# Matrix-engine order in an expert mixture: scheduled, or as the kernel writes it from the second pair of experts on

## The chip, the cores and the metric

The kernel runs on one core of a Trainium2 chip. The metric is device time in microseconds (us) of that core, from launch to end; each kernel is run several times and the median counts. A profile, taken of one execution, records every instruction. PE is TensorE (matrix engine), PEld its weight load, DVE VectorE, ACT ScalarE, POOL GpSimd, SP SyncE, which here issues the loads.

## The reference

A two-layer encoder on 512 tokens of 1024 channels, float32. Layer 0 mixes tokens by a Fourier transform and a convolution, layer 1 by banded attention; each layer ends with an expert-choice mixture of 16 experts, where each expert takes its own 64 tokens. The change is in the mixture:

```
def ec_moe(h, router_w, router_b, w_gate, w_up, w_down):
    aff = softmax(h @ router_w + router_b)
    gate, idx = top_k(aff transposed, 64)             # 64 tokens an expert
    xg = h[idx]                                       # 16 x 64 x 1024
    hid = silu(xg @ w_gate) * (xg @ w_up)             # 1024 x 1024 weights, each expert its own
    y = (hid @ w_down) * gate
    return zeros.at[idx].add(y)
...
x = x + gate_c * ec_moe(rms_norm(x) * (1 + scale) + shift, ...)
```

All three weight matrices of all 16 experts are read once a layer: 48 matrices of 4 MiB, 201.3 MB.

## The kernel before

`moe` (line 859) works through eight pairs of experts (`for pr in range(NP)`, line 1031). The two experts of a pair have 64 tokens each, so the 128 x 128 array is split in column halves: expert i = 0 uses columns 0 to 63, i = 1 columns 64 to 127. For a pair the source writes, in this order:

1. **gate**: `expert_mm` (line 965) with `wg_d`, into two banks of PSUM (one for each half of the 1024 outputs), then ACT's SiLU into `sg` (line 1040);
2. **combine** of the pair before (`combine_all`, line 1019): 16 matmuls that put the weighted outputs `Y` back on the tokens, which DVE adds to `x` (line 1017);
3. **up**: `expert_mm` with `wu_d`;
4. **ahead** (line 1044): `onehot` (DVE line 903, POOL line 909), `gather` (line 920; DVE line 928 and ACT line 926 empty its banks) and `weights` (lines 937 to 944) of the *next* pair;
5. DVE multiplies `up` with `sg` (line 1064), PE transposes the product (line 1069), `evac` (lines 151, 153) puts it into `hid`;
6. **down**: `expert_mm` with `wd_d`, then `y_out` (lines 1007 to 1009: DVE, ACT, DVE) forms `Y`.

The last pair's down projection is done in pieces (`down_piece`, line 981: one of 512 columns, two of 256), each followed by its part of combine.

One `expert_mm` has four steps of two chunks, one chunk for each expert; a chunk is 2 x 128 rows of a weight matrix, 1 MiB. Each step has eight matmuls, in the source with i = 0 and i = 1 by turns:

```
for kk in range(2):
    for h in range(2):
        for i in range(2):
            matmul(ps[h][64*i:64*i+64], lhs[:, k, 64*i:64*i+64], w[i].row(kk)[:, 512*h:512*h+512])
```

So a pair has 24 chunks, a layer 192; numbered from 0 in the order in which PE uses them, the second pair's up projection (`pr` = 1) begins with chunk 32 and the last pair's up projection ends with chunk 183.

`chunk` (line 100) issues each load on SP's queue, into one of the mixture's 15 slots of 1 MiB (`w0` to `w10`, `3a`, `3b`, `4a`, `4b`; `Slot`, line 54). Slots are handed out in rotation when the program is written, so a load waits on SP until PE has finished with the chunk that had the slot 15 places earlier, and all later loads wait behind it.

What the source fixes is which instructions there are and which data they depend on. The order on each engine is set by a scheduler that runs when the program is built (`schedule_with_timeline_sim=True`, line 1480): it plays the program through a model of the engines and issues on each engine what the model finds ready first. It is not bound to the source's order, for PE, DVE, ACT, POOL or SP.

Of the kernel before, what the change touches and what calls it, by code (L numbers as in the profile page):

```python
# [21 lines left out]
EPS = 1e-6  # L22
# [10 lines left out]
def trunk(ctx: ExitStack, tc: tile.TileContext, x_d, c_d, pos_d, ada_w, ada_b, mix_g, ffn_g, w_in,  # L33
# [7 lines left out]
    free_banks, free_slots = list(range(8)), [f"w{i}" for i in range(SLOTS)]  # L41

    class Bank:
        """One bank of PSUM, given back after its last use."""
# [9 lines left out]
    class Slot:  # L54
        """8 KB a partition, for a chunk of weights or parts of it, given back after its last use."""
# [14 lines left out]
    def area(i, n, dt=FT):  # L70
        """1a, 2a: 12 KB; 1b, 2b: 4 KB; 0a to 4b else: 8 KB, the 3s and 4s slots in the mixtures."""
        return pool.tile([P, n], dt, name=i if i[0] in "034" else f"area{i}")
# [6 lines left out]
    def row_tmp():  # L79
        """Of a slot lent for it, where there is one."""  # L80
        if not extra:
            return tmp()
        extra.append(extra.pop(0))
        return extra[-1]
# [15 lines left out]
    def chunk(src):  # L100
        """One chunk of weights in the order of the stream."""
        w = Slot()
        loads[0] = nc.sync.dma_start(w.cut(src.shape[1]), src)
        return w
# [7 lines left out]
    def halves(w, eng=None):  # L112
        """w = hi + lo exactly, both of 12 significant bits."""
# [10 lines left out]
    def behind(*ins):  # L124
        """Bulk work that its engines take up only after these instructions."""
# [13 lines left out]
    def mm3(ps, l, r, start, stop):  # L139
        """float32 product of (hi, lo) operands: the three parts above 2**-24."""  # L140
# [6 lines left out]
    def evac(out, in_):  # L147
        """PSUM to SBUF, by turns on the two engines that read PSUM."""
# [100 lines left out]
    def ada_steps(l, s, j, pool_too=False):  # L249
        """The same block in steps, on VectorE, or on ScalarE and GpSimd."""  # L250
# [45 lines left out]
    def row_half(p, col, h):  # L296
        """A half of a column vector of 1024 (128 x 8) as a row, the same on all partitions."""
# [11 lines left out]
    # the router's weights, 16 of 32 columns; the sum over the four groups of its rows  # L309
# [17 lines left out]
    def rsqrt(y, v, n, scale):  # L327
        """y = scale / sqrt(v): a guess from the bits, a step of third and one of second order."""
# [21 lines left out]
    def norm_rows(ss, name, parts=2, t0=0, n=TT):  # L350
        """1/sqrt(mean(x**2) + EPS) for some tiles of tokens, from the sums over parts of the channels"""
# [8 lines left out]
    def rms_row(rbc, ss, name, parts=2):  # L360
        """1/rms of the tokens as a row, the same on all partitions"""
# [7 lines left out]
    def h_area():  # L369
        """h as hi + lo, [128 channels, 512 tokens] eight times"""  # L370
# [3 lines left out]
    def h_parts(src, f, rbc, hi, lo, a, sh, k):  # L374
        """h = x*rbc*a + sh as hi + lo, x as [128 channels, 512 tokens]"""
# [4 lines left out]
    def fourths(*tags, dt=FT):  # L380
        """Areas as [128, 512] four times each"""
        return [m[:, S * k:S * k + S] for m in [area(i, 2048, dt) for i in tags] for k in range(4)]

    def turned_x():
        """x as [128 channels, 512 tokens] eight times"""
        return fourths("0a", "0b")
# [5 lines left out]
    def add_gated(t, h, ps, eng):  # L392
        """x += gate * y, of one token tile and one half of the channels."""
# [6 lines left out]
    def mixer0():  # L400
# [19 lines left out]
        # the first three chunks come by halves of their rows, the first halves ahead of the blocks 1 and 3  # L420
# [70 lines left out]
        def conv(ct, split):  # L491
            """Some taps on ScalarE and GpSimd, the others on VectorE"""
# [36 lines left out]
        def spectrum(g, u):  # L529
            """The real part of the transform of one group, u its projection"""  # L530
# [40 lines left out]
        # LayerNorm over the 512 channels, which lie across partitions  # L571
        ones = one.to_broadcast([P, 32])

        def sums(src):
            """Four rows (32 times each) of sums over the channels of four tiles"""
# [15 lines left out]
        # The order of the steps, one letter a kind (the branches below say which), its number, the engine or the  # L591
        # split of the step after a dot, the free slots that it picks after a colon.
# [122 lines left out]
    def prefix_matrices():  # L715
        """Rows j, columns i: 1 where j <= i; where j < i"""
# [9 lines left out]
    class Router:  # L726
# [20 lines left out]
        def part(self, t, h):  # L747
            """one tile of tokens, half of its channels: the sum of squares, the logits' part"""
# [17 lines left out]
        def affinities(self, t0, n):  # L766
            """softmax over the experts for some tiles of tokens, turned to a row an expert"""
# [34 lines left out]
        def tops(self, wk, out):  # L802
            """The 64 largest of a row, in steps"""
# [15 lines left out]
        def slots(self):  # L819
            """idx[token, expert]: 1..64, the token's place among the expert's, or 0  # L820

            Taken are the tokens above the 64th largest, and as many of its equals, the first ones, as are left."""
# [14 lines left out]
            with Bank() as p0, Bank() as p1:  # L837
                # counts of a mask up to each token (z = 0) and before it (z = 1)
# [20 lines left out]
    def moe(rt, last, meanwhile):  # L859
        l, a, sh, aff = rt.l, rt.a, rt.sh, rt.aff  # L860
        A0 = [area(i, 2048) for i in ("0a", "0b")]
        # the tokens as they come to the mixture: x itself until the first outputs are added to it
# [16 lines left out]
        def room():  # L879
            """For the transposed one-hot matrices and the weighted outputs."""  # L880
# [6 lines left out]
        def first_onehot():  # L887
            """The one of the first pair by its parts, straight with the factors."""
# [8 lines left out]
        def onehot(pr):  # L897
            """The one-hot matrix of a pair of experts."""
# [14 lines left out]
        def gather(pr, hf):  # L913
            """Half of the channels of the gathered rows of a pair of experts."""
# [569 lines left out]
```

## Time and profile before

| | us |
|---|---|
| median of 3 runs (1574.2 to 1575.35) | 1574.2 |
| profiled execution: span, first to last instruction | 1573.9 |
| of which PE busy | 1452.2 (92%) |
| DVE / ACT / POOL busy | 638.0 / 338.8 / 312.1 |
| share of the chain that ended last: PE / DVE | 78% / 16% |
| mixture of layer 0, from the first gather to the last piece's output | about 272 to 786 |
| mixture of layer 1, likewise | about 1052 to 1560 |

No time of the profiled execution apart from its span is recorded; the 0.3 us between its span and the median is less than the spread of the runs. A chain row gives start, length and what ran. A chain "x64" of line 976 stands for one `expert_mm`: 32 matmuls, each recorded as two rows. A window row gives for one stretch the busy time of each engine, then the clock granted to TensorE (1.00 is 2.4 GHz, 0.50 is 1.2 GHz), the DMA engines' busy share and the GB/s that they moved (the share can pass 1 by a little).

### The profile page before, as it was taken

What the parts mean: (1) busy time and instruction counts of PE and PEld (TensorE: products, weight loads), DVE (VectorE), ACT (ScalarE), POOL (GpSimd) and SP (SyncE); (2) the same over time, 40 slices, a digit from 0 to 9 for tenths busy, and PEclk for the clock granted to TensorE, in tenths of its full rate; (3) what the DMA queues carried; (4) which work ended last, traced back from release to release, by engine and by line L of the source; (5) the groups of instructions that cost most, each with busy time, mean ns of one, the idle gap of its engine ahead of it and who ended that gap; (6) DMA issues with size and microseconds to landing.
All of it is one profiled execution on the core that took longest, in us unless ns stands there. A gap on an engine that the chain in (4) does not pass through costs nothing.

```text
span 1573.9 us, 18049 instructions
## 1 busy us (share of the span) xinstructions
PE 1452.2 (92%) x7203; PEld 789.1 (50%) x7203; DVE 638.0 (41%) x1165; ACT 338.8 (22%) x686; POOL 312.1 (20%) x234
## 2 busy tenths in 40 slices
PE   5994897999999999999888989979999999999995
PEld 3762574544454444444467666654455344444443
DVE  5599946121221211211268888560222212212114
ACT  3443432210010000000255653411110010010002
POOL 2597631200000000000156655300000000000002
PEclk8997898999999999999989999979999999999998
DMA  9465389789998999999810476578999998999991
GB/s 339 141 221 182 128 316 405 303 330 403 410 401 343 355 383 362 412 362 406 276 36 14 120 228 199 213 310 321 386 390 412 410 378 318 409 362 404 371 388 69
DMA packets 158428, 480.69 MB, mean 305 GB/s; under 512 B 10416, under 2 KB 31176, under 8 KB 158344
## 3 DMA queue, kind: packets, MB, share of 16 engines
q1 hardware_dynamic: 158264, 479.27, 80.0%
q8 instruction: 57, 0.93, 0.2%
q0 software_dynamic: 80, 0.26, 0.0%
q14 instruction: 27, 0.22, 0.0%
HBM read 477.40 MB, written 2.10 MB: 305 GB/s over the span
## 4 chain that ended last, share of the span: by engine, by line
PE 78%; DVE 16%; ACT 2%; issue 1%; DMA 1%; SPq 0%; POOL 0%; ACTq 0%; DVEq 0%; POOLq 0%
PE bank L976 45%; PE bank L920 8%; DVE 0b L506 7%; PE bank L1014 4%; PE bank L141 3%; PE bank L142 3%; PE bank L143 3%; PE bank L997 2%; PE bank L227 2%; PE bank L1301 1%; DMA 4a<-in_fc_w_in_dram 1%; PE bank L942 1%; DVE nm L1271 1%; PE bank L1267 1%; PE bank L1292 1%
## 5 line engine op out<-in xcount | busy, mean ns | idle before, releaser
L976 PE MATMUL bank<-w,area2b 128*64 128x512 f32 x744 | 221.5, 598 | 0.0
L976 PE MATMUL bank<-w,area1b 128*64 128x512 f32 x688 | 207.3, 597 | 0.0
L976 PE MATMUL bank<-w,area1a 128*64 128x512 f32 x624 | 159.1, 594 | 0.9 <-ACT area2b L926 0.6
L909 POOL TENSOR_TENSOR tmp<-tmp,rr 128x512 f32<-128x512 f32 x14 | 17.7, 1265 | 650.6 <-DVE tmp L903 628.9
L1017 DVE TENSOR_TENSOR x<-x,bank 128x512 f32<-128x512 f32 (+1 forms) x136 | 81.1, 652 | 145.6 <-PE bank L1014 145.4
L976 PEld LDWEIGHTS bank<-w,area2b 128*64 128x64 f32 x744 | 67.8, 136 | 107.0 <-issue 101.7
L976 PEld LDWEIGHTS bank<-w,area1b 128*64 128x64 f32 x688 | 64.9, 136 | 106.0 <-issue 102.0
L1007 DVE SCALAR_TENSOR_TENSOR tmp<-bank,af,gbc 128x512 f32<-128x512 f32 (+1 forms) x34 | 24.5, 719 | 217.6 <-PE bank L976 191.1
L119 POOL TENSOR_TENSOR w<-w,w 128x1024 fp32r<-128x1024 f32 x30 | 75.5, 2536 | 148.7 <-ACT w L118 142.6
L1064 DVE TENSOR_TENSOR area1a<-bank,area1a 128x512 f32<-128x512 f32 x32 | 22.1, 691 | 198.0 <-PE bank L976 198.0
L976 PEld LDWEIGHTS bank<-w,area1a 128*64 128x64 f32 x624 | 55.7, 137 | 72.5 <-issue 68.5
L1014 PE MATMUL bank<-area2a 128*128 128x512 f32 (+1 forms) x272 | 73.4, 401 | 12.1 <-ACT area2a L1008 12.1
L1014 PEld LDWEIGHTS bank<-area2a 128*128 128x128 f32 x272 | 45.3, 188 | 56.7 <-ACT area2a L1008 22.2
L506 DVE SCALAR_TENSOR_TENSOR 0b<-3b,cw,0b 128x512 f32<-128x512 f32 x60 | 69.0, 1186 | 0.1
L920 PEld LDWEIGHTS bank<-tmp,0a 128*128 128x128 f32 x384 | 52.3, 191 | 33.4 <-issue 33.3
L1008 ACT ACTIVATE area2a<-tmp 128x512 fp32r<-128x512 f32 (+1 forms) x34 | 20.6, 607 | 219.7 <-DVE tmp L1007 219.7
L920 PE MATMUL bank<-tmp,0a 128*128 128x128 f32 x384 | 66.5, 286 | 0.0
L928 DVE TENSOR_SCALAR area1b<-bank,a,mod 128x128 f32<-128x128 f32 x32 | 13.1, 409 | 123.6 <-PE bank L920 118.7
L920 PE MATMUL bank<-tmp,0b 128*128 128x128 f32 x384 | 61.5, 279 | 0.0
L141 PE MATMUL bank<-area1a,w 128*128 128x512 f32 x132 | 52.8, 420 | 7.1 <-ACT area1a L377 6.3
L920 PEld LDWEIGHTS bank<-tmp,0b 128*128 128x128 f32 x384 | 51.2, 192 | 11.4 <-issue 11.4
L143 PE MATMUL bank<-area1a,w 128*128 128x512 f32 x132 | 53.4, 406 | 1.2 <-POOL w L119 1.2
(466 smaller groups left out, 2639.2 us busy)
## 6 DMA issues: line engine op xcount, KB each, us to landing
w<-in_moe_w_gate_dram SPq DMA_DIRECT2D x93, 1024.0 KB, 10.5
w<-in_moe_w_up_dram SPq DMA_DIRECT2D x86, 1024.0 KB, 12.9
w<-in_moe_w_down_dram SPq DMA_DIRECT2D x85, 1024.0 KB, 7.6
w<-in_ada_w_dram SPq DMA_DIRECT2D x44, 1024.0 KB, 7.0
3b<-in_moe_w_up_dram SPq DMA_DIRECT2D x10, 1024.0 KB, 13.9
4b<-in_moe_w_gate_dram SPq DMA_DIRECT2D x9, 1024.0 KB, 12.0
4a<-in_moe_w_gate_dram SPq DMA_DIRECT2D x9, 1024.0 KB, 10.6
3a<-in_moe_w_up_dram SPq DMA_DIRECT2D x9, 1024.0 KB, 11.8
```

What stands on the lines that cost most here:

```text
L119: eng.tensor_sub(lo.ap[:, s], w.ap[:, s], hi.ap[:, s].bitcast(FT))
L141: nc.tensor.matmul(ps, l[0], r[0], start=start, stop=False)
L142: nc.tensor.matmul(ps, l[0], r[1], start=False, stop=False)
L143: nc.tensor.matmul(ps, l[1], r[0], start=False, stop=stop)
L227: nc.tensor.matmul(ps[32 * q:32 * q + 32], cond[:, 4 * half + q], w[:, q], start=half == 0, stop=half == 1)
L506: nc.vector.scalar_tensor_tensor(cv, g[:, k:k + S], wt(k), cv, op0=OP.mult, op1=OP.add)
L920: nc.tensor.matmul(p[:, P * q:P * q + P], src_x(t, 4 * hf + q), oh[:, P * t:P * t + P], start=t == 0, stop=t == TT - 1)
L976: nc.tensor.matmul(ps[h][CAP * i:CAP * i + CAP], lhs[:, k, CAP * i:CAP * i + CAP], w[i].row(kk)[:, 512 * h:512 * h + 512], start=k == 0, s ...
L997: nc.tensor.matmul(ps[CAP * i:CAP * i + CAP, :n], lhs[:, k, CAP * i:CAP * i + CAP], w[i][:, kk], start=k == 0, stop=k == KT - 1)
L1007: nc.vector.scalar_tensor_tensor(f, ps[:, :n], af, gbc[:, s], op0=OP.mult, op1=OP.mult)
L1014: nc.tensor.matmul(p[:, :n], ohT[:, P * t:P * t + P], Y[z][:, c0:c0 + n], start=z == 0, stop=z == 1)
L1017: nc.vector.tensor_add(xx, xx, p[:, :n])
```

## The change

Around the loop over pairs, from `pr` = 1 to the end of the last pair's transposes, PE's instructions are put under a manual schedule: the scheduler keeps them, on PE alone, in the order in which the source writes them. The first pair, the pieces of the last down projection, and the other four engines remain with the scheduler, which, however, now plays its model with another PE. Both mixtures run through this code. The edit also takes out docstrings and comments, which issue nothing; lines after 1030 stand 3 to 4 lower.

```
         pend = None
+        order = ExitStack()
         for pr in range(NP):
+            if pr == 1:
+                order.enter_context(tc.manual_schedule(engines={mybir.EngineType.PE}))
             if pr:
                 xg, ohT, af = nxt
...
                             nc.scalar.activation(frozen[2 * t + h], xx, AF.Copy)
+        order.close()
         ss = small("fss", 3 * TT, 1)
```

What it moves, first on PE at the start of the fourth pair's gate projection in layer 0. (Left of the arrow stands the bank, right of it the weights and the gathered tokens `area2b`; `3b`, `w6` are chunks of expert i = 0, `w10`, `w3` of i = 1.) Before:

```order
L976 MATMUL bank3_2717<-3b_2719,area2b_1839 64x512
L976 MATMUL bank7_2718<-3b_2719,area2b_1839 64x512
L976 MATMUL bank3_2717<-w10_2721,area2b_1839 64x512
L976 MATMUL bank7_2718<-w10_2721,area2b_1839 64x512
L976 MATMUL bank3_2717<-3b_2719,area2b_1839 64x512
L976 MATMUL bank3_2717<-w10_2721,area2b_1839 64x512
L976 MATMUL bank7_2718<-3b_2719,area2b_1839 64x512
L976 MATMUL bank7_2718<-w10_2721,area2b_1839 64x512
L976 MATMUL bank3_2717<-w6_2731,area2b_1839 64x512
L976 MATMUL bank7_2718<-w6_2731,area2b_1839 64x512
L1014 MATMUL bank5_2769<-area2a_2010 128x512
L1014 MATMUL bank2_2777<-area2a_2010 128x512
```

With the change:

```order
L976 MATMUL bank3_2719<-3b_2721,area2b_1839 64x512
L976 MATMUL bank3_2719<-w10_2723,area2b_1839 64x512
L976 MATMUL bank7_2720<-3b_2721,area2b_1839 64x512
L976 MATMUL bank7_2720<-w10_2723,area2b_1839 64x512
L976 MATMUL bank3_2719<-3b_2721,area2b_1839 64x512
L976 MATMUL bank3_2719<-w10_2723,area2b_1839 64x512
L976 MATMUL bank7_2720<-3b_2721,area2b_1839 64x512
L976 MATMUL bank7_2720<-w10_2723,area2b_1839 64x512
L976 MATMUL bank3_2719<-w6_2733,area2b_1839 64x512
L976 MATMUL bank3_2719<-w3_2735,area2b_1839 64x512
L976 MATMUL bank7_2720<-w6_2733,area2b_1839 64x512
L976 MATMUL bank7_2720<-w3_2735,area2b_1839 64x512
```

Before, the two matmuls of `3b` stand together, then the two of `w10`, and after the first two of `w6` the combine of the pair before cuts in (line 1014). Now i = 0 and i = 1 alternate throughout, and combine and gather stand behind whole projections; PE's order on the change is the source's in every pair from the second on.

Second, on DVE late in layer 0's mixture, around the product of gate and up. Before:

```order
L1017 TENSOR_TENSOR x_61<-x_61,bank6_3587 128x512
L928 TENSOR_SCALAR area2b_1839<-bank2_3653,a01_119,mod01_108 128x128 x2
L928 TENSOR_SCALAR area2b_1839<-bank0_3674,a01_119,mod01_108 128x128 x2
L943 COPY af_3701<-bank6_3702 64x1
L944 COPY af_3701<-bank6_3702 64x1
L1017 TENSOR_TENSOR x_61<-x_61,bank3_3595 128x512
L1017 TENSOR_TENSOR x_61<-x_61,bank7_3591 128x512
L1064 TENSOR_TENSOR area1a_1837<-bank4_3599,area1a_1837 128x512
L1064 TENSOR_TENSOR area1a_1837<-bank5_3600,area1a_1837 128x512
L151 COPY area1a_1837<-bank7_3711 128x512
```

With the change (line 1064 is now line 1067):

```order
L1017 TENSOR_TENSOR x_61<-x_61,bank3_3597 128x512
L1067 TENSOR_TENSOR area1a_1837<-bank4_3601,area1a_1837 128x512
L1067 TENSOR_TENSOR area1a_1837<-bank5_3602,area1a_1837 128x512
L928 TENSOR_SCALAR area2b_1839<-bank2_3655,a01_119,mod01_108 128x128 x2
L928 TENSOR_SCALAR area2b_1839<-bank0_3676,a01_119,mod01_108 128x128
L943 COPY af_3703<-bank6_3704 64x1
L944 COPY af_3703<-bank6_3704 64x1
L928 TENSOR_SCALAR area2b_1839<-bank0_3676,a01_119,mod01_108 128x128
L151 COPY area1a_1837<-bank7_3713 128x512
```

Before, the gathered rows (line 928) are emptied ahead of the product; now the product stands first and the gather's banks are emptied behind it. All eight additions of combine stand ahead of both.

Third, SP's loads for the third pair in layer 0. Before:

```order
L103 DMA 4a_2573<-in_moe_w_up_dram 128x2x1024
L103 DMA 4b_2575<-in_moe_w_up_dram 128x2x1024
L103 DMA w9_2489<-in_moe_w_gate_dram 128x2x1024
L103 DMA w2_2491<-in_moe_w_gate_dram 128x2x1024
L103 DMA 3a_2537<-in_moe_w_up_dram 128x2x1024
L103 DMA w8_2539<-in_moe_w_up_dram 128x2x1024
L103 DMA 3b_2549<-in_moe_w_up_dram 128x2x1024
L103 DMA w10_2551<-in_moe_w_up_dram 128x2x1024
L103 DMA w6_2561<-in_moe_w_up_dram 128x2x1024
L103 DMA w3_2563<-in_moe_w_up_dram 128x2x1024
```

With the change:

```order
L103 DMA w9_2491<-in_moe_w_gate_dram 128x2x1024
L103 DMA w2_2493<-in_moe_w_gate_dram 128x2x1024
L103 DMA 3a_2539<-in_moe_w_up_dram 128x2x1024
L103 DMA w8_2541<-in_moe_w_up_dram 128x2x1024
L103 DMA 3b_2551<-in_moe_w_up_dram 128x2x1024
L103 DMA w10_2553<-in_moe_w_up_dram 128x2x1024
L103 DMA w6_2563<-in_moe_w_up_dram 128x2x1024
L103 DMA w3_2565<-in_moe_w_up_dram 128x2x1024
L103 DMA 4a_2575<-in_moe_w_up_dram 128x2x1024
L103 DMA 4b_2577<-in_moe_w_up_dram 128x2x1024
```

Two up chunks (`4a`, `4b`), which PE uses last in their projection, stood ahead of two gate chunks; now the loads stand in the order in which PE uses them. With one like piece in layer 1 this is all that moves on SP; POOL's order is the same.

## Rows read from the trace of the kernel before

**Rows 1.** The page: the span, and PE's share of it

```profile
span 1573.9 us, 18049 instructions
PE 1452.2 (92%) x7203; PEld 789.1 (50%) x7203; DVE 638.0 (41%) x1165; ACT 338.8 (22%) x686; POOL 312.1 (20%) x234
```

**Rows 2.** Chain that ended last, second pair of layer 0: start, us, what ran

```profile
349.39 3.85 PE bank L1014 x16
353.24 13.88 PE bank L976 x64
367.12 7.34 PE bank L920 x64
376.62 1.43 PE bank L976 x5
```

**Rows 3.** The same chain, from one steady pair of layer 0 to the next

```profile
623.03 13.89 PE bank L976 x60
653.80 1.86 PE bank L976 x4
658.16 3.58 PE bank L976 x12
688.98 13.89 PE bank L976 x60
```

**Rows 4.** SP's waits, in total, times, longest; and the size of a load

```profile
SPq L103 <- PE bank L976: 749.8, 237, 23.2
w<-in_moe_w_gate_dram SPq DMA_DIRECT2D x93, 1024.0 KB, 10.5
```

**Rows 5.** Windows: PE, PEld, DVE, ACT, POOL busy; clock, DMA share, GB/s

```profile
386.00:480.00 94.00, 93.42 (x428) 42.05 (x424) 21.86 (x35) 8.44 (x16) 2.71 (x2) 1.00 1.02 407
612.00:623.00 11.00, 11.00 (x50) 4.87 (x47) 1.76 (x5) 2.11 (x4) 0.00 (x0) 1.00 0.66 236
1170.00:1275.00 105.00, 104.64 (x480) 47.26 (x475) 23.75 (x38) 8.16 (x15) 2.71 (x2) 1.00 1.03 411
```

**Rows 6.** SP's queue where a load follows an idle stretch

```profile
322.76 0.88 SPq L103 DMA_DIRECT2D w<-in_moe_w_up_dram  x2
1101.18 3.80 SPq L103 DMA_DIRECT2D w<-in_moe_w_up_dram  x3
```

**Rows 7.** Windows of layer 0

```profile
318.00:322.00 4.00, 4.00 (x22) 1.29 (x18) 0.00 (x0) 2.19 (x4) 2.28 (x4) 1.00 0.04 15
322.76:353.24 30.48, 30.48 (x166) 15.39 (x164) 8.40 (x17) 4.78 (x9) 1.04 (x1) 1.00 0.96 373
353.24:739.00 385.76, 381.51 (x1751) 173.71 (x1752) 80.26 (x136) 30.80 (x57) 6.78 (x5) 1.00 0.97 384
```

**Rows 8.** The chain and windows of layer 1

```profile
1131.89 13.88 PE bank L976 x64
...
1098.00:1101.00 3.00, 3.00 (x18) 1.00 (x16) 0.00 (x0) 1.94 (x4) 2.06 (x4) 1.00 0.00 0
1101.18:1131.89 30.71, 30.71 (x168) 15.61 (x166) 8.93 (x18) 4.29 (x8) 1.04 (x1) 1.00 0.96 371
1131.89:1513.00 381.11, 376.92 (x1745) 173.53 (x1745) 79.65 (x135) 30.69 (x57) 6.78 (x5) 1.00 0.98 386
```

**Rows 9.** DVE's timeline: the last pair's product, layer 0 and layer 1

```profile
752.59 0.69 DVE L1064 TENSOR_TENSOR area1a<-bank,area1a 128x512 f32<-128x512 f32 x1 [12.46 <-PE bank L976]
1533.00 0.69 DVE L1064 TENSOR_TENSOR area1a<-bank,area1a 128x512 f32<-128x512 f32 x1 [12.46 <-PE bank L976]
```

**Rows 10.** End of layer 1: its last weights' window, and PE's last piece

```profile
1513.00:1536.00 23.00, 22.77 (x102) 9.16 (x101) 3.45 (x5) 1.79 (x3) 0.00 (x0) 1.00 1.07 367
1555.61 2.81 PE bank L997 x16
```

**Rows 11.** Windows in which PE waits, for the clock

```profile
271.00:276.00 5.00, 3.48 (x16) 3.51 (x17) 2.76 (x10) 0.00 (x0) 2.05 (x3) 0.50 1.03 409
757.00:777.00 20.00, 17.18 (x87) 9.23 (x84) 6.12 (x10) 4.69 (x12) 0.00 (x0) 1.00 1.05 349
```

More of the change, by code (lines that the diff above doesn't have):

```diff
@@ L1030, in moe @@
         pend = None
+        order = ExitStack()
         for pr in range(NP):
+            if pr == 1:
+                order.enter_context(tc.manual_schedule(engines={mybir.EngineType.PE}))
             if pr:
@@ L1089, in moe @@
                             nc.scalar.activation(frozen[2 * t + h], xx, AF.Copy)
+        order.close()
         ss = small("fss", 3 * TT, 1)
```

## Prediction

> **What bounds the kernel now.** I read the page first. PE is busy for 1452.2 of 1573.9 us [rows 1], but a busy share does not tell whether PE does useful work or works at half its worth, so I went to the chain that ended last and compared one pair of experts with another. In the second pair of layer 0, combine (3.85 us), the up projection (13.88), the gather (7.34) and 2.16 us from the gather's end to the next projection (376.62 - 374.46, weights and transposes) stand end to end without a gap [rows 2]. From one steady pair to the next, however, 688.98 - 623.03 = 65.95 us pass [rows 3]. Add up what a pair needs when each piece runs as in rows 2: three projections of 13.88, plus 3.85, 7.34 and 2.16, is 55.0 us. So 10.9 us of a steady pair are PE time that the work does not need.
>
> Rows 3 show where most of it goes. A step of a projection, eight matmuls (16 rows), takes a quarter of 13.88, 3.47 us, when the two column halves alternate. Where the scheduler issued two matmuls of one half first and the rest later, the step takes 1.86 + 3.58 = 5.44 us, 1.97 more. A steady pair has this in the four steps of its gate projection: 7.9 us. The other 3.0 are the switches to combine and gather in between, and combine waiting for its inputs right after the down projection.
>
> Then the loads. A pair brings 24 chunks of 1 MiB [rows 4], 25.2 MB. Where nothing holds them up they run at 407 GB/s over 94 us and 411 over 105 us, with the DMA engines' share at 1.02 and 1.03 [rows 5]. I take 409: 61.5 us a pair. In the steady pairs there is a stretch with the share at 0.66 and 236 GB/s [rows 5]; SP's longest total wait, 749.8 us, is for PE at the projections' line [rows 4]. So in the steady pairs PE sets the pace (65.95), the slots are full, and the loads stand still for lack of a free slot.
>
> **What the change does, part by part.**
>
> *PE's order.* No instruction is added or removed. In each pair from the second on the split steps close up (7.9 us), combine goes behind the gate projection, so that DVE's and ACT's work on `Y` lies beside 13.88 us of PE work instead of ahead of it, and the gather goes behind the up projection. PE's need falls from 65.95 to 55.0 us. That is not the gain: the pair cannot be shorter than its loads, 61.5. Next late is a weight chunk.
>
> *Waits that the order adds.* A waiting matmul now holds all behind it on PE. The gather waits for the one-hot rows (DVE, POOL), issued right after the down projection two projections earlier: nothing. The transposes wait for DVE's product, two operations of 0.69 [rows 9], which now stand ahead of the gather's evacuations on DVE and lie beside 7.34 us of gather: nothing. The rest, evacuation of the transposes, lies in the 2.16. If these covers fail, the pair has 61.5 - 55.0 = 6.5 us before it shows, so I bound this cost between 0 and 10.9 a pair and take 0.
>
> *SP's order.* It now follows PE's use, so the newest load is never one that PE needs later than the next. I price this at nothing: the slots stay 15 and the bytes the same. POOL and ACT gain and lose nothing that PE waits for.
>
> *The sum, layer 0.* I count chunks. At 318 to 322 us the DMA is idle (share 0.04), and the first load after it, at 322.76, is chunk 32, so 32 have landed [rows 6, 7]. From there to 353.24, where the second pair's up projection begins [rows 2], 30.48 us at 373 GB/s bring 10.8 more. From 353.24 to 739.00 the trace moves 385.76 us x 384 GB/s = 148.1 MB, 141 chunks [rows 7]: so at 739 all 184 chunks up to the last pair's up projection have landed, 13.6 us before DVE's product at 752.59 [rows 9]. At 409 GB/s the same bytes take 362.1 us and land at 715.3. The last step's matmuls follow (3.47): product at 718.8. PE alone would be ready earlier: 367.12, where the second pair's up ends, plus six pairs of 55.0 is 697. Gain 752.59 - 718.8 = **33.8 us**.
>
> *Layer 1.* The same: DMA at 0 from 1098 to 1101, chunk 32 issued before it and chunk 33 after it, so 33 landed; 30.71 us x 371 GB/s bring 10.9 by 1131.89, where up begins [rows 6, 8]. 381.11 us x 386 GB/s = 147.1 MB, 140 chunks, land by 1513, 20 us before the product at 1533.00 [rows 8, 9]. At 409 GB/s they take 359.7 us: 1491.6, product at 1495.1; PE alone 1145.8 + 330 = 1476. Gain **37.9 us**.
>
> *What follows the product moves as a block.* Eight chunks come behind the last up projection; in layer 1 they take 23 us at 367 GB/s [rows 10]. PE begins its last piece at 1555.61, 22.6 us after the product, which itself comes 3.5 after the last up chunk: 26.1 us against 23. So the pieces hardly wait; likewise in layer 0, and the attention between the mixtures depends on the first one's end and keeps its order. What is left over: bytes moved are not chunks landed, as several loads are in flight; half a chunk a layer, 1.3 us, I take off twice. 33.8 + 37.9 - 2.6 = 69.1 us. The profiled execution (span 1573.9) and the median (1574.2) agree within the spread of the runs, so I take it off the median: **1505 us**.
>
> A rule that speaks against this: rows 5 show 407 and 411 GB/s. The Trainium skill (DMA: Bandwidth & Descriptors, Specifications) gives a core's share of the memory as about 358 GB/s. By it a pair's loads would take 70.3 us, more than the present 65.95, and the change would gain nothing. The trace does not agree (the loads already run faster than that for 100 us), so the rate of the rows stands.
>
> **The rivals.**
>
> *The loads don't stay full (0.20).* The mean between the marks is now 384 and 386 GB/s. If pauses remain, because PE holds slots through the 9.5 us of gather and transposes, or because a pair's first loads are issued late, the rate may rise only half way, to 397. For it: the pauses of layer 0's first pair stand before the change's reach. Against: once PE is ahead, the slots are mostly free. Landing then at 353.24 + 373.0 = 726.2 and 1131.89 + 370.5 = 1502.4, products at 729.7 and 1505.9, gain 22.9 + 27.1 = 50: 1524 us.
>
> *PE waits in order for as long as it saved (0.05).* That takes 10.9 us of waits a pair, for one-hot rows, SiLU or an evacuation, with nothing allowed to pass. For it: the scheduler moved work forward for just such waits. Against: the pieces of rows 2 run in the source's order without a gap. 1574 us.
>
> *TensorE's clock falls in the new waits (0.07): slower.* PE will wait for chunks by 6.5 us a pair, in pieces between steps. Where PE is thin, the granted clock is at 0.50, the 1.2 GHz level: 271 to 276 us, busy 3.48 of 5.00 after an idle stretch [rows 11]. If one projection a pair ran at that level, a pair would need 55.0 + 13.9 = 68.9 us, 2.95 more than now; for the six pairs from product to product in each layer 35 us: 1609 us. It decides from 10.9 us, four fifths of one projection, a pair. Against: from 757 to 777 PE is busy for 17.18 of 20 us and the clock stays at 1.00 [rows 11]; the forecast has PE busy for 55.0 of 61.5. The Trainium skill (TensorE: Matmul & The Clock Gate, Loop structure matters more than you think) warns of this loop, in which each burst of matmuls waits for a load and the engine goes cold; by that rule the rival would be the likeliest, by the row it is not.
>
> That the change doesn't do what it says I leave out: PE's built order is the source's from the second pair on.
>
> **How the numbers follow.** Forecast 0.68, the half-way loads 0.20, no change 0.05, slower 0.07; a measurement of this kernel can tell about 0.2%, 3 us, from no change. So faster 0.88, same 0.05, slower 0.07. The forecast's own bounds: at 411 GB/s and without the half chunks 75 us, 1499; a little below that, if the pieces gain too: 1496. The upper end takes in the half-way loads and the same few us: 1528. What is left out is 0.12 and the tails.
>
> **What would show it right or wrong.** Right: a pair 61 to 62 us long in the later pairs of both layers; DMA share above 1 from the second pair to the last piece; each projection 13.9 us or stretched only by waits for a load; PE's idle time before line 976 put down to DMA; SP's wait for PE far below 749.8; the first product after 353 unchanged, the last ones at about 719 and (less the first layer's gain) 1461. Wrong: pairs of 66 with the DMA share dipping still (slots), idle PE released by DVE, ACT or POOL (order), or a clock below 1.00 inside the mixtures.

## The result, and the profile after

The median fell from 1574.78 to **1507.26 us** (1504.48 to 1508.68, four runs each); the ratio is 0.957, 95% interval 0.9554 to 0.9581. The forecast was 1505, its range 1496 to 1528. The page of the changed kernel, beside [rows 1, 4] (the third line is a kind of load: count, size, median us from issue to landing):

```profile
span 1507.0 us, 18064 instructions
...
PE 1367.3 (91%) x7203; PEld 764.9 (51%) x7203; DVE 635.7 (42%) x1165; ACT 337.7 (22%) x686; POOL 312.0 (21%) x234
...
w<-in_moe_w_gate_dram SPq DMA_DIRECT2D x93, 1024.0 KB, 18.1
```

PE does the same 7203 rows in 1367.3 us instead of 1452.2: 84.9 us less. The span lost 66.9, so PE stands idle 18 us longer than before. The chain that ended last shows what. First the second pair of layer 1 (combine, up, gather, then down and the next gate without a break), then a later pair of layer 0:

```profile
1098.64 3.87 PE bank L1014 x16
1102.50 13.88 PE bank L976 x64
1116.39 7.34 PE bank L920 x64
...
1126.47 27.69 PE bank L976 x128
...
548.11 8.61 PE bank L976 x39
556.72 18.41 DMA w<-in_moe_w_gate_dram
...
577.20 18.24 DMA w<-in_moe_w_up_dram
...
595.49 3.65 PE bank L976 x14
```

The gate projection is whole: 27.69 us is down and gate at 13.85 each, and the rows of 1.86 and 3.58 us of [rows 3] are gone. In the later pairs the chain leaves PE twice a pair, through a weight chunk still on its way. The windows of these stretches (columns as in [rows 5]), the last one a stretch in which PE waits:

```profile
354.50:480.00 125.50, 124.55 (x656) 58.76 (x656) 29.52 (x50) 10.05 (x19) 2.71 (x2) 1.00 1.02 408
...
530.00:700.00 170.00, 157.91 (x820) 75.97 (x818) 33.23 (x58) 14.12 (x27) 2.71 (x2) 1.00 1.03 411
...
1133.00:1478.00 345.00, 332.64 (x1696) 155.43 (x1693) 76.28 (x128) 29.13 (x54) 6.77 (x5) 1.00 1.03 409
...
618.00:637.00 19.00, 16.32 (x74) 5.89 (x70) 4.15 (x5) 1.26 (x2) 1.36 (x1) 1.00 1.03 414
```

The loads run at 408 to 411 GB/s without a pause where before they had a mean of 384 and 386 [rows 7, 8], and the granted clock stays at 1.00, the 2.4 GHz level, while PE waits. The waits turned round accordingly. SP's total for PE at the projections' line fell from 749.8 us [rows 4] to 439.4, and the weight loads of PE now wait for DMA (second row: layer 0's mixture alone; total, times, longest; before, this wait was 0.4 us there):

```profile
SPq L103 <- PE bank L976: 439.4, 172, 22.5
...
PEld bank L976 <- DMA w<-in_moe_w_up_dram: 12.5, 10, 2.4
```

DVE's timeline gives the end of each layer's last up projection, to be held against [rows 9]:

```profile
721.61 0.69 DVE L1067 TENSOR_TENSOR area1a<-bank,area1a 128x512 f32<-128x512 f32 x1 [14.18 <-PE bank L976]
...
1468.14 0.69 DVE L1067 TENSOR_TENSOR area1a<-bank,area1a 128x512 f32<-128x512 f32 x1 [14.76 <-PE bank L976]
```

The starts of the eight products of a layer on this timeline give the seven intervals from pair to pair, which all that follows is read by (us; "sum" is first to last product, in layer 1 in the last column):

| kernel | 1 | 2 | 3 | 4 | 5 | 6 | 7 | sum, layer 0 | sum, layer 1 |
|---|---|---|---|---|---|---|---|---|---|
| before | 56.4 | 64.1 | 73.8 | 65.9 | 66.0 | 66.0 | 50.5 | 442.6 | 444.4 |
| after | 56.5 | 55.3 | 55.6 | 58.8 | 61.1 | 62.0 | 61.2 | 410.4 | 408.9 |
| e2, four and four | 58.5 | 57.4 | 57.6 | 57.4 | 57.7 | 62.6 | 61.2 | 412.5 | 409.9 |
| e5, one cut, uneven | 59.4 | 59.4 | 59.6 | 59.4 | 59.6 | 59.4 | 58.5 | 415.4 | 417.5 |
| e6, one cut, even | 57.5 | 57.6 | 57.8 | 57.6 | 58.8 | 61.3 | 61.7 | 412.3 | 409.9 |
| e7, fewer loads | 56.4 | 55.3 | 55.5 | 55.3 | 55.5 | 55.3 | 55.5 | 388.8 | 388.8 |
| e9, two cuts, uneven | 73.4 | 66.3 | 66.4 | 66.4 | 66.5 | 66.4 | 48.2 | 453.5 | 456.8 |
| e10, two cuts, even | 66.6 | 59.5 | 59.6 | 59.5 | 59.6 | 59.5 | 52.5 | 416.9 | 415.9 |

After has two regimes in each layer: three or four intervals at about 55.5 us, PE's own pace, while it eats the chunks that lie ready in the slots (55.5 us at 408 GB/s bring 21.6 chunks, and a pair takes 24); then 61 to 62 us, the pace of the loads.

The account of the 66.9 us: 442.6 - 410.4 = 32.2 and 444.4 - 408.9 = 35.5 between the products; 1.2 lost ahead of the first mixture, which the change doesn't touch (first product at 311.2 instead of 310.0; in the eleven runs below it lies between 307.9 and 310.2); 1.6 lost between the mixtures, nearly all in the pieces; 2.0 gained behind the last product (1507.0 - 1468.1 = 38.9 against 40.9). The last two are not shown to be effects of the change: in e1 to e10, all of which leave the pieces to the scheduler as after does, the stretch between the mixtures' products is 335.2 to 337.7 us (before 336.0, after 337.6) and the last one 38.8 to 42.0.

### The profile page after: what moved, and what is told of

Its sections match the earlier page's. It is cut to its first block, busy times and chain, and to the rows that moved or that the text cites. A ratio compares the mean times of both kernels' runs of the same rounds, so it can differ in the third digit from the quotient of the medians.

```text
span 1507.0 us, 18064 instructions
## 1 busy us (share of the span) xinstructions
PE 1367.3 (91%) x7203; PEld 764.9 (51%) x7203; DVE 635.7 (42%) x1165; ACT 337.7 (22%) x686; POOL 312.0 (21%) x234
## 4 chain that ended last, share of the span: by engine, by line
PE 62%; DVE 17%; DMA 16%; ACT 2%; issue 1%; SPq 1%; POOL 0%; DVEq 0%; ACTq 0%; POOLq 0%
PE bank L976 32%; PE bank L920 8%; DVE 0b L506 7%; DMA w<-in_moe_w_up_dram 6%; DMA w<-in_moe_w_gate_dram 5%; PE bank L141 3%; PE bank L142 3%; PE bank L143 3%; PE bank L997 3%; PE bank L1014 3%; DMA 4b<-in_moe_w_gate_dram 2%; PE bank L227 2%; DMA 4a<-in_moe_w_up_dram 1%; PE bank L1305 1%; DMA 4a<-in_fc_w_in_dram 1%
## 5 line engine op out<-in xcount | busy, mean ns | idle before, releaser
L976 PE MATMUL bank<-w,area2b 128*64 128x512 f32 x744 | 194.3, 595 | 9.4 <-DMA w<-in_moe_w_gate_dram 6.5
L976 PE MATMUL bank<-w,area1b 128*64 128x512 f32 x688 | 182.0, 595 | 7.1 <-DMA w<-in_moe_w_up_dram 4.3
L976 PEld LDWEIGHTS bank<-w,area2b 128*64 128x64 f32 x744 | 62.0, 137 | 109.1 <-issue 85.4
L976 PEld LDWEIGHTS bank<-w,area1b 128*64 128x64 f32 x688 | 58.8, 137 | 106.6 <-issue 84.6
L1014 PE MATMUL bank<-area2a 128*128 128x512 f32 (+1 forms) x272 | 64.2, 386 | 5.1 <-ACT area2a L1008 5.1
L1043 ACT ACTIVATE area1a<-bank 128x512 f32<-128x512 f32 x32 | 19.2, 599 | 195.4 <-PE bank L976 195.4
L920 PE MATMUL bank<-tmp,0a 128*128 128x128 f32 x384 | 59.8, 278 | 0.0
L926 ACT ACTIVATE area1b<-bank,mod,a 128x128 f32<-128x128 f32 x32 | 14.6, 457 | 184.3 <-DVE area1b L928 184.3
L920 PEld LDWEIGHTS bank<-tmp,0a 128*128 128x128 f32 x384 | 50.5, 192 | 9.7 <-issue 9.7
## 6 DMA issues: line engine op xcount, KB each, us to landing
w<-in_moe_w_gate_dram SPq DMA_DIRECT2D x93, 1024.0 KB, 18.1
```

What stands on the lines that cost most here:

```text
L920: nc.tensor.matmul(p[:, P * q:P * q + P], src_x(t, 4 * hf + q), oh[:, P * t:P * t + P], start=t == 0, stop=t == TT - 1)
L976: nc.tensor.matmul(ps[h][CAP * i:CAP * i + CAP], lhs[:, k, CAP * i:CAP * i + CAP], w[i].row(kk)[:, 512 * h:512 * h + 512], start=k == 0, s ...
L1014: nc.tensor.matmul(p[:, :n], ohT[:, P * t:P * t + P], Y[z][:, c0:c0 + n], start=z == 0, stop=z == 1)
```

## The experiments

All start from the kernel after. Medians of four runs each, the ratios are to the kernel before on the same chip.

| run | edit | us | ratio, 95% interval |
|---|---|---|---|
| e1 | two of four gate steps: one expert's four matmuls, then the other's | 1509.0 | 0.9566 to 0.9594 |
| e2 | all four gate steps so | 1508.8 | 0.9562 to 0.9591 |
| e3 | combine mid-gate, gather mid-up, between steps | 1511.9 | 0.9584 to 0.9613 |
| e4 | the change from the seventh pair on alone | 1545.8 | 0.9796 to 0.9829 |
| e5 | combine inside the gate's steps after 2 matmuls | 1519.2 | 0.9632 to 0.9661 |
| e6 | combine inside the gate's steps after 4 | 1509.9 | 0.9576 to 0.9605 |
| e7 | a quarter of the loads left out | 1465.8 | 0.9290 to 0.9321 |
| e8 | the change from the first pair on | 1507.6 | 0.9557 to 0.9586 |
| e9 | gather inside the gate's steps after 2 and 8 | 1597.4 | 1.0127 to 1.0157 |
| e10 | gather inside the gate's steps after 4 and 8 | 1519.6 | 0.9629 to 0.9661 |
| e11 | source order through the last pieces too | 1516.3 | 0.9614 to 0.9642 |

**Is it the order within a step? (e1, e2)** The prediction said that a step takes 3.47 us when the column halves alternate. These two take the alternation away and leave all else.

```
+ apart = wd is wg_d and first is None          # e1: and c < 2
+ for m in range(8):
+     i, kk, h = (m // 4, m // 2 % 2, m % 2) if apart else (m % 2, m // 4, m // 2 % 2)
- for kk in range(2):
-     for h in range(2):
-         for i in range(2):
```

> After, but in the first two of the four steps of each gate projection, from the second pair on, the four matmuls of one expert (one half of TensorE's columns) are issued first and the four of the other expert behind them, so that the halves no longer alternate. Nothing else changes. Theory (split steps cost PE time, and a pair is as long as the longer of PE's need, 55.0 us, and its loads, 61.4): a matmul of one half alone takes half of 1.86 us, eight of them 7.44 at most, or 6.5 where the two in the middle overlap, against 3.47; two steps add 6.1 to 7.9 us, so a pair needs 61.1 to 62.9 us of PE. From the second pair on all seven pairs of a layer take that instead of 58.5 on average: 36 to 61 us more than after, 1543 to 1568 us. Rival (the gain came from moving combine and gather, and the order within a step does not matter): 1507 us, within 3.

> The same with all four steps of each gate projection from the second pair on. Theory: 12.1 to 15.9 us more of PE a pair, 67.1 to 70.9 us, above the 65.95 of before: 1627 to 1680 us, slower than before although combine and gather stay where the change put them. PE never waits for a load, and the DMA share falls below 0.95. Rival (the moves are the gain): 1507 us, within 3.

Both missed by far. The chain of e2, a down and a gate projection in one:

```profile
435.04 29.76 PE bank L976 x128
```

29.76 instead of 27.69 us: four split steps cost 2.1 us together, not 12 to 16. In e1, with two split steps, the same stretch is hardly shorter:

```profile
378.55 29.57 PE bank L976 x128
```

So the price does not grow with the number of split steps; it is paid once. PE's timeline of e2 shows how the gate projection begins (`3b` is of expert i = 0, `w` here of i = 1):

```profile
448.80 2.31 PE L976 MATMUL bank<-3b,area2b 128*64 128x512 f32 x5
450.52 0.64 PE L976 MATMUL bank<-w,area2b 128*64 128x512 f32 x1
450.94 0.59 PE L976 MATMUL bank<-3b,area2b 128*64 128x512 f32 x1
451.00 0.59 PE L976 MATMUL bank<-w,area2b 128*64 128x512 f32 x1
```

For 1.7 us one half runs alone; from then on the two run side by side, although four matmuls of one stand ahead of four of the other. So alternation is not what counts. The time stayed at 1509 all the same, since 57.5 us of PE a pair is still less than the loads take: the intervals are 57.5 until the loads become the bound, then 61 to 62.

**Is it the place of combine and gather? (e3)**

```
-expert_mm([g0, g1], xg, wg_d, e, None ...)
-combine_all(pend)
+expert_mm([g0, g1], xg, wg_d, e, lambda: combine_all(pend))      # called between the second and third step
...
+def early(): onehot(pr + 1); gather(pr + 1, 0); gather(pr + 1, 1)
+expert_mm([u0, u1], xg, wu_d, e, early)
```

> After, but combine stands in the middle of the gate projection again and the gather of the next pair in the middle of the up projection, as the scheduler of before placed them, between whole steps: no step is split. Theory: this costs the switches only, at most the 3.0 us a pair that before shows beside the split steps; PE needs 55.0 to 58.0 us a pair, still below the loads' 61.4: 1507 to 1512 us, and later pairs of 61 to 62 us. Rival (the moves are the gain): pairs go back toward 65.95 and the time to 1540 to 1575 us.

As the theory has it. In the chain the gather stands between the two halves of an up projection. The row ahead of it is the second half of the gate and the first half of up, 13.88 us as for a whole projection; the half behind it takes 7.02 us instead of 6.94, so the switch costs 0.1 us:

```profile
346.58 13.88 PE bank L976 x64
360.46 7.34 PE bank L920 x64
367.81 7.02 PE bank L976 x32
```

The early steady intervals are 55.5 to 56.0 us, later ones 60 to 62. The median lies 4.6 us above after's, of which the profiled executions show 1.9 between the products; where the rest lies I can't say.

**Then what did a split step cost? (e5, e6)** New theory: the two halves work on what is queued for each, and a matmul over all columns (combine, gather) waits until both are empty. Then the longer half between two such matmuls counts, and 2 matmuls of one half alone, then foreign work, then 2 and 4, is 2 + 4 turns instead of 4.

```
 for kk in range(2):
+    if kk == 1: combine(pend, c, 0); combine(pend, c, 512)        # e6: after 2 + 2 matmuls
...
+    # e5: in kk == 0 the order is i0 h0, i0 h1, [the two combines], i1 h0, i1 h1
-combine_all(pend)
```

> After, but combine is cut into four pieces of four matmuls that stand inside the four steps of the next gate projection, each after the first two matmuls of a step, which both lie in one half of TensorE's columns: two matmuls of that half and none of the other, then combine, then two of the one and four of the other, as in the split steps of before. The second and third run showed that the order within an undisturbed step costs little (four of one half and then four of the other: a down and a gate projection back to back take 29.79 us instead of 27.69). New theory (the two halves work side by side on what is queued for each, and a matmul over all columns must wait until both have run empty, so what counts is the longer half between two such matmuls: 2 + 4 = 6 turns of 0.9 us instead of 4): 1.97 us a step, 7.9 us a pair. PE needs 55.5 + 7.9 = 63.4 us, in the last pair without a gather 56; that is above the loads' 61.4. Six pairs and the last make 436 us from the first product to the last of a layer, against 410 now: 26 us twice, and up to 2 us a pair for the switches: 1555 to 1585 us. Rival (a split step costs nothing by itself; before was slow through the order of its loads or its gathers): 1507 to 1512 us.

> The same pieces of combine in the same four steps, each after the first four matmuls of a step, two of either half. New theory: the halves run empty together, 2 + 2 = 4 turns as in a whole step, so only the switches are paid: 1507 to 1513 us. Rival (any cut of a step costs what before showed): like the fifth run, 1555 to 1585 us.

e6 came as expected, e5 did not: 1519. Its chain, from the end of a down projection on:

```profile
391.93 0.75 DVE tmp L1008
...
393.28 2.06 DVE area2a L1010 x2
...
395.87 3.63 PE bank L977 x16
399.51 1.13 PE bank L1015 x4
...
410.15 17.31 PE bank L977 x76
```

I had cut each step once only. Between two pieces of combine lie the uneven rest of one step (2 and 4) and the uneven start of the next (2 and 0): eight matmuls, four of either half, 3.63 us. Only the last rest is bare: 17.31 us for 76 rows, where e6 has

```profile
408.46 15.60 PE bank L978 x72
```

1.71 us a pair, and 59.5 - 57.6 = 1.9 in the intervals. (e5's row has two matmuls more because its pieces stand two matmuls earlier; that saves nothing at the start, where its two matmuls of one half take as long, 1.8 us, as e6's four.) One more row of e6 prices the unevenness:

```profile
394.29 3.58 PE bank L978 x16
```

Eight matmuls, four of either half, between two pieces of combine take 3.58 us, exactly what six uneven ones took in before. Both runs also pay a second, smaller price. `Y` is ready only some 3.4 us after the end of down (the DVE groups), and combine's first piece has two or four matmuls of the gate to hide behind and not a whole projection. Those matmuls and three of the piece's own fill most of the 3.4 us; PE stands idle for 0.7 (e5, 380 to 700 us; total, times, longest):

```profile
PE bank L1015 <- DVE area2a L1010: 3.6, 5, 0.7
```

e6 has the same wait, and with the switches its pair takes 57.6 us instead of 55.5. e5's time follows its pace: 58.4 to 60.4 us in every interval, the loads never quite the bound, 417.5 us instead of 408.9 in layer 1.

**The scheduler's pattern, rebuilt (e9, e10).** Before cut a step twice, after its second matmul and at its end (the rows of 1.86 and 3.58 in [rows 3]). So do these, with the gather. (In before's steady pairs the fourth gate step is not cut at its end: its rest runs on into up, and there the 30 matmuls that are left take 13.89 us, as long as 32 in an even projection. The sum stays at 7.9 us.)

```
 for c in range(4):
     ...
+    # e9: i0 h0, i0 h1, next(within), i1 h0, i1 h1, then kk = 1;   e10: kk = 0, next(within), kk = 1
+    next(within)                                   # four of the gather's 32 matmuls
```

> After, but the gather of the next pair is cut into eight pieces of four matmuls that stand inside the gate projection of the second to seventh pair: one after the first two matmuls of each step, which both lie in one half of TensorE's columns, and one at the step's end, so that each step runs as 2 matmuls, gather, 6 matmuls, gather, which is how before ran its split steps. The fifth run cut a step in one place only, and the uneven rests of two steps ran together as eight even ones. Theory (the halves run empty before a matmul over all columns, and the longer half counts: 2 + 4 turns instead of 4): 1.97 us a step, 7.9 us a pair: rows of 1.86 and 3.58 us in all four steps, steady pairs of 55.5 + 7.9 = 63.4 us. From the first product of a layer to the last 55.5 + 7.3 + 7.9 (the first has two gathers) + 5 x 63.4 + 48.2 (the last has none) = 436 us instead of 410: 26 us twice, about 1560 us, 1550 to 1570. Rival (foreign work inside a step costs only its switches): 1507 to 1515 us.

> The same eight pieces of the gather in the same four steps, the first of a step behind its first four matmuls, two of either half, the second at its end: 4, gather, 4, gather. Theory: 2 + 2 turns, nothing lost but the switches; the loads stay the bound: 1507 to 1513 us, later pairs of 61 to 62 us. Rival (a cut costs wherever it stands): as the ninth run.

First a step of e9, then one of e10 (chain; L998 is the projection here, L937 the gather):

```profile
470.49 3.58 PE bank L998 x12
474.07 1.09 PE bank L937 x8
475.15 1.86 PE bank L998 x4
```

```profile
456.61 1.87 PE bank L998 x8
458.48 1.09 PE bank L937 x8
459.56 1.87 PE bank L998 x8
```

The same eight matmuls and the same foreign work: 1.86 + 3.58 = 5.44 us where the cut leaves 2 and 6, 1.87 + 1.87 = 3.74 where it leaves 4 and 4. Six matmuls of 2 and 4 take as long as four turns of one half; two matmuls of one half take as long as four of both. The intervals differ by 66.4 - 59.6 = 6.8 us, four times 1.70, and the times by 78 us, since 66.4 is above the loads' pace and 59.6 below it. The windows of one stretch show that, e9 first:

```profile
400.00:700.00 300.00, 290.74 (x1307) 127.46 (x1306) 59.97 (x102) 24.98 (x46) 6.77 (x5) 1.00 0.97 382
```

```profile
400.00:700.00 300.00, 291.68 (x1472) 128.52 (x1472) 64.59 (x111) 26.23 (x48) 5.42 (x4) 1.00 1.03 411
```

e9's 66.4 is near before's 65.95, with its load rate of 382 (before 384). PE is "busy" for 97% in both windows: its busy share can't tell the two apart. The Trainium skill (TensorEngine Tiling (Array Packing), Key Properties) says both halves of this: tiles work independently, and a change of the tiling mode empties the engine. These rows agree, and add the price.

What e9 and before share is the rows of 1.86 and 3.58, four times 1.97 us; the other 3 us of a pair are of another make in either (in before the switches and PE's waits for `Y` and for DVE's product, for e9 see below), so that the totals come so near is in part chance. e9 is slower than before as a whole because its first interval is split too (73.4 us, with two gathers; before 56.4). And its loads stand in the order of use, gate, up, down, as after's do: the gain is gone all the same, so the new order of loads is not what pays.

Both expectations missed in time (1597 for 1560, 1520 for 1510), in the same term: the base. In order, the gather's first piece waits for its one-hot rows, which DVE forms after `Y` and POOL after that. In e10, from the end of down to the first piece of the gather, and then PE's wait there (380 to 700 us; total, times, longest):

```profile
452.55 0.75 DVE tmp L1031
...
454.04 1.36 POOL tmp L909
455.45 1.16 PE bank L937 x8
```

```profile
PE bank L937 <- POOL tmp L909: 6.3, 5, 1.3
```

The one-hot rows come 2.9 us after the end of down; the gate's first four matmuls fill the first 1.6 of that, and PE stands idle for 1.3. Combine's wait for a free bank adds 0.4, the even cuts 3.74 - 3.47 = 0.27 a step, 1.1 a pair, and the gather in eight pieces takes 1.16 + 7 x 1.09 = 8.8 us instead of 7.34, 1.5 more. That is the 59.6 - 55.4 = 4.2 us between e10's interval and an uncut one.

**Are the later pairs bound by loads? (e7)**

```
+once = first is None and c % 2 == 1
+w = [chunk(src[0])] * 2 if once else [...]          # both experts use the first one's chunk
```

> After with a quarter of the loads left out: from the second pair on (in the down projections of all pairs but the first), in every second step of a projection both experts use the chunk of the first one, so that part of the weights is not the right one. All matmuls stay. Theory (after is bound by its loads in the later pairs): 18.9 MB a pair take 46 us at 410 GB/s, so PE sets the pace with 55.5 us in every pair and 48 to 51 in the last: the last product of layer 0 comes at 311 + 6 x 55.5 + 48 = 692 instead of 721.6, that of layer 1 some 24 us earlier in its own layer: about 1454 us, 1448 to 1462. Rival (the later pairs of 61 to 62 us are stretched by slots, evacuations or PE's order and not by bytes): 1500 us or more.

The last product of layer 0 comes at 698 us, where 692 was expected:

```profile
698.35 0.69 DVE L1071 TENSOR_TENSOR area1a<-bank,area1a 128x512 f32<-128x512 f32 x1 [11.43 <-PE bank L980]
```

All matmuls are there, and each interval from the second on, the later ones too, is 55.3 or 55.5 us. So the stretch to 61 or 62 in after comes from the loads, and PE's need is 55.4. Leaving loads out also asks less of the slots, so e7 alone does not part bytes from slots; the windows do. After moves 411 GB/s with the DMA engines' share at 1.03 in its later pairs; e7, where PE sets the pace:

```profile
600.00:700.00 100.00, 99.20 (x499) 44.01 (x495) 22.10 (x37) 9.43 (x16) 1.93 (x2) 1.00 0.92 343
```

The time is 4 us above the expected range because I gave the last interval 48 to 51 us; it holds a gather like the others (the last pair's own) and takes 55.5, 4.5 to 7.5 us more a layer.

**How the gain spreads over the pairs (e4)**

```
-if pr == 1:
+if pr == NP - 2:
     order.enter_context(tc.manual_schedule(...))
```

> The change from the seventh of the eight pairs on alone: the first six are left to the scheduler. Theory (PE works ahead on loaded chunks until the slots run empty, then loads are the bound): before, all chunks up to the last up projection had landed 13.6 us (layer 0) and 20 us (layer 1) ahead of the product, and a pair lost 3.6 to 3.9 us of load time. Two pairs in order win at most 2 x 10.9 = 21.8 us on PE, and as far as loads allow 13.6 - 3.5 + 2 x 3.9 = 18 us in layer 0, and 20 - 3.5 + 2 x 3.6 = 23.7 in layer 1, so 18 and 21.8: about 40 us of the 67, 1535 us. Rival (each pair in order wins its share): 67 x 2/7 = 19 us, 1556 us.

1545.8: 29 us saved, between the theory's 40 and the rival's 19. From the sixth product to the last it takes 103.8 us in layer 0 (before 116.4) and 105.5 in layer 1 (120.6). In layer 0 the loads end it, as expected (the second fence is a window of before, columns as in [rows 5]):

```profile
717.45 18.85 DMA w<-in_moe_w_up_dram
```

```profile
660.00:690.00 30.00, 30.00 (x144) 15.08 (x142) 4.05 (x10) 3.62 (x7) 0.00 (x0) 1.00 0.90 347
```

But the load time that two pairs lose was sized too high: in before's last two the loads run at 410 or 411 GB/s but for this stretch, an estimated 4.6 us at 410 and not 2 x 3.9. That leaves 14.7 of the 18 us; the other 2 I can't account for. In layer 1 PE and not a load ends it, and there I had priced both pairs at 10.9 us, where before's last interval is 54.7 and not 65.95: its gate projection has no gather to be split by. Two of the seven pairs still hold 43% of the gain, so it does not add up pair by pair; but e4 alone does not prove the stock of chunks. The two regimes of after, with the loads at the same rate in both, do.

**Wider, for a faster version (e8, e11)**

```
-if pr == 1:                 +if pr == 0:                      # e8
-order.close()  (before the pieces)      +order.close()  (behind them)     # e11
```

> After with PE's source order from the first pair on instead of the second. Theory (from the second pair on the loads run without a pause, so the first pair matters only through the slots that it frees and the pauses of the loads while it runs, share 0.23 at 318 to 323 us): a few us either way, 1502 to 1512 us. Rival (in the first pair PE has to wait for one-hot rows, the mean and the gate's row, which the scheduler fills with steps of a projection; in order the wait is bare): 5 to 20 us a layer, 1517 to 1547 us.

> After with PE's source order kept through the last pair's three pieces of the down projection as well, up to the end of the mixture. Theory (the pieces in after wait for their loads, which land at the rate of the loads, or run on PE without a gap): nothing to gain but a switch or two, 1504 to 1509 us. Rival (in order, a piece's combine waits bare for the weighted outputs, 1.5 to 2.5 us each, which the next piece's matmuls fill now): 2 to 5 us a layer, 1511 to 1517 us.

e8 is no different from after. e11 is 9 us slower, in its rival's direction: its stretch from the last product of layer 0 to the first of layer 1 is 6.7 us longer than after's and the one behind the last product 5.3, against the 2 to 5 that the rival gave. In layer 0 the loss stands between the second and the third piece, in e11 and then in after (chain; L1114 and L1115 are the transposes of the new `x`):

```profile
742.29 0.49 DVE tmp L1007
...
745.32 0.44 PE bank L1014 x2
745.78 0.43 DVE x L1017
746.26 0.69 PE bank L1114 x2
...
750.20 6.66 PE bank L997 x32
```

```profile
745.69 0.50 DVE tmp L1007
...
748.49 3.60 PE bank L997 x24
```

In order, PE goes through combine, DVE's addition and the transposes tile by tile and waits in each, which the rival did not name; the third piece begins 7.9 us after the second's outputs were ready to be weighted (742.29 us), in after 2.8 (745.69). The scheduler puts the piece's matmuls over the additions. No version that keeps all the loads was found to be faster than after.

## Why the prediction was right

- **The bound.** PE set the pace before and the loads after, as forecast: intervals of 61.1 to 62.3 us against 61.5 forecast, 408 to 411 GB/s against 409. e7 shows it by taking loads away, with the DMA share of 1.03 beside it.
- **PE's need.** 55.0 us forecast from [rows 2], 55.4 measured (e7, and after's early pairs).
- **The split steps.** The size held, 5.44 against 3.47 us, and e9 brings the old interval back. The reason was half wrong: "a quarter of 13.88, 3.47 us, when the two column halves alternate". Giving up the turns costs 2.1 us a pair, not 7.9 (e2). What costs is work over all columns inside a step, at a place where the halves are uneven (e9 against e10). The forecast did not suffer, since the source's order has neither.
- **The sum.** 33.8 and 37.9, less 1.3 each: 32.5 and 36.6 forecast, 32.2 and 35.5 measured between the products. The blocks behind them did not move quite rigidly: 1.6 us lost in layer 0's pieces, 2.0 gained at the end, 1.2 lost ahead of the mixture. 69.1 forecast, 66.9 in the profile, 67.5 in the medians. The points in time came less near: the last products at 721.6 and 1468.1 us, forecast at 718.8 and 1461. That the sum misses by 2 us and not by 7 owes something to luck: the 2.6 us held back for half a chunk a layer (between the products 1.6 and 2.4 were missing, but no run shows that half chunks are the reason), and the 2.0 at the end, which was not forecast.
- **Order waits at nothing.** Right for this change: the gather's one-hot rows and combine's `Y` each have at least a whole projection to hide behind. e5, e6, e9, e10 and e11 show them as soon as that cover is shorter: PE idle for 0.7 us a pair (combine's `Y`) or 1.3 (one-hot rows), and 9 us in all for the pieces.
- **The rivals.** Loads at half the gain (397 GB/s) fell: 408 to 411. A falling clock fell: 1.00 in the stretches in which PE waits. The Trainium skill's rule (TensorE: Matmul & The Clock Gate, Loop structure matters more than you think) speaks of a long wait before every matmul and does not bite here; the trace shows PE busy for 16.32 of 19 us in such a stretch, at a granted clock of 1.00. Nor does the 358 GB/s a core of the Trainium skill (DMA: Bandwidth & Descriptors, Specifications): the trace has 411 over 170 us.

## What to carry to other kernels

When TensorE is used in column halves, count between two matmuls over all columns how many each half gets: the longer half is the price, and a busy share of 97% says nothing about it. A busy engine's order is worth fixing by hand where each wait has a whole block of work to hide behind, and was better left to the scheduler where it has not (the pieces, 9 us). And before forecasting what a shorter step saves, work out what the next resource needs for the same unit of work: here 10.5 of PE's microseconds a steady pair were to be had (65.95 - 55.4), and 4.6 an interval were kept (32.2 / 7).

## What was not expected of the hardware

The two column halves run side by side even when four matmuls of one stand in the queue ahead of four of the other: 29.76 us for 64 matmuls against 27.69 with strict turns. And six matmuls, two of one half and four of the other, take as long between two matmuls over all columns as eight evenly split ones, 3.58 us. A load of 1 MiB takes a median of 18.1 us from issue to landing in after, where the loads run without a pause, 10.5 in before and 8.5 in e7, where they pause (share 0.85 to 0.92). At 410 GB/s 18.1 us are 7.4 MB, by estimate some seven loads under way at once; so here the time to landing tells how many loads are under way and not how fast the bytes move.
